# State-space layer of a two-layer trunk: mask products and a sum moved from GpSimd to VectorE, the modulation's running sums divided differently over the groups

## Chip, core and metric

The kernel runs on one core of a Trainium2 chip. The metric is device time in microseconds (us) of one execution. Engines: PE is TensorE, DVE is VectorE, ACT is ScalarE, POOL is GpSimd, SP is SyncE, which here issues DMAs. They run side by side and wait for one another through semaphores; each works off its own instructions strictly in program order.

## What is computed

A trunk of two layers for 512 tokens of width 1024. Each layer makes six rows of modulation from a vector c, runs a mixer and then a mixture of experts. The mixer of the second layer, which the change concerns, is a state-space layer with 8 groups of 4 heads, cut into 4 chunks of 128 tokens:

```
mod = silu(c) @ ada_w[layer] + ada_b[layer]          # shift1, scale1, gate1, shift2, scale2, gate2
z, xbc, dt = split(modulate(rmsnorm(x)) @ w_in)
xs, B, C   = split(silu(conv4(xbc) + conv_b))
x_dt   = xs * softplus(dt + bias);  a_cs = cumsum(dt * A) in each chunk
y_diag = (C B^T * exp(a_cs_l - a_cs_s), lower triangle) x_dt        # the mask product
y_off  = C prev * exp(a_cs)                                         # prev: scan over the chunks' states
y = y_diag + y_off + xs * D                                         # the sum of y's parts
g = y * silu(z);  g = g * rsqrt(mean(g*g over the group's 256) + eps) * norm_w
x = x + gate1 * (g @ w_out)
```

## The kernel before

All of the state-space layer is in `odd_mixer`. A loop over g = 0 to 8 does in each turn the dense products and the convolution of group g and the later steps of group g - 1. Tokens lie along the free axis (512), channels on the partitions; a group has 256 channels of x and z, in two tiles q = 0, 1, and 128 each of B and C.

Of one group, in the order in which the program writes it:

- `conv`: a dense product (pdb, pdc, pdx; 24 matmuls of 128x512 each, since weights and activations are split into a high and a low part, L449 to L452; low parts by L112), then four taps of the convolution: the first on ACT (L1592), three on DVE (L1595, 511, 510 and 509 columns wide), then Silu on ACT (L1598), which may need the loading of a table. The next weights' splits (names b2h, b2l for the B columns of group 2) are made meanwhile.
- `decay` and `masked`: ms, the decays exp(a_cs_l - a_cs_s) for four heads and one chunk, 128x512, on ACT (L1631, L1633); then ms times cbm, the product C B^T under the triangle (L1618). Four of these multiplications a group (L1646): before, chunks 0 and 2 on POOL, 1 and 3 on DVE.
- `xtok`: x turned to tokens on PE (pxd, L1659), times dt (xdt, L1662) and times the decay to the chunk's end (xw, L1665) on DVE.
- `states`: pst on PE (L1673) from xw, and the scan prev on ACT and DVE.
- `ymm`: y_diag into pyd (L1692) and y_off into pyo (L1696) on PE; `zgate`: z and its Silu zt (L1703).
- `assemble`: yy = D x + pyd (L1711, DVE), yt = pyo times the decay (L1714, DVE), yy + yt (L1716, POOL, 128x384), times zt into gT (L1718, L1720, DVE); squares on ACT, and their sum gsum on POOL (L1727).
- `gnorm`, of two groups at a time: pgn (L1733, PE, sums over channels), gv (L1736, DVE), Ln (L1738) and Exp (L1739) on ACT, each with a table load, three steps on DVE to gy (L1741 to L1743), a broadcast of a row over the partitions, gb, on POOL (L1746), and gT times it on DVE (L1749).

Woven in is the modulation of this layer: a11 and a12 are generators (`ada`) that make columns 2048 to 4095 of mod (gate1, shift2) and 4096 to 6143 (scale2, gate2), here called its two halves. Each keeps a running sum over 8 weight tiles on DVE (L204 the first, L202 the seven others, 128x2048 each) and ends with a row sum on PE (L212), an addition on DVE (L215) and stores by SP (L221, L223); the second half also prepares the router, with reloading mc (L244) and plb on PE (L249). The list `fill` holds their 20 steps in order, and OFILL[g] says how many are taken at the end of group g; what is left runs at the end of group 7.

After that `gate_row` loads gate1 (L463) into the same buffer (tag "rows", one buffer) that the second half's rows occupied. `out_proj` multiplies g with w_out in 16 steps of 128 rows: SP loads a step's weight rows (sor, L484) two steps ahead, DVE scales them by the gate (L492), ACT and DVE split them (sow0h, sow0l and so on, L111, L112) and g (gs), and PE adds up 24 products (so, L457 to L459). With it come expert weights for the next part on the same SP queue.

What sets the order of instructions: they are written in the order above, and a scheduler with estimated durations then orders each engine's program; tables on ACT are kept in order by explicit dependencies (`in_order`). The trace's order is thus the program's order and not one made on the chip.

Of the kernel before, what the change touches and what calls it, by code (L numbers as in the profile page):

```python
# [20 lines left out]
P = 128  # L21
# [38 lines left out]
NTMP = 2  # L60
TAIL = 2
FILL = (0, 1, 5, 0, 1, 0, 1, 1, 1, 2, 1, 0, 0, 1, 0, 5, 4, 0, 0, 1, 1, 1, 4, 0, 12)
OFILL = (4, 0, 5, 4, 4, 0, 3, 4)
LO = {"v": "V", "e": "VVG", "m": "V", "o": "V", "s": "VV"}
FPOOL = (0,)
FSTEPS = "x0 h0 x1 h0 x2 h1 h1 h1 h0 x3 h2 h2 h3 h2 h3 h3"
# [10 lines left out]
def trunk_kernel(ctx, tc, x, c, ada_w, ada_b, norm1_w, norm2_w, mix_w_in, pool_w, pool_scale,  # L77
# [4 lines left out]
    V, S, GP, PE, SP = nc.vector, nc.scalar, nc.gpsimd, nc.tensor, nc.sync  # L82
# [1372 lines left out]
    def odd_mixer(layer, prev):  # L1455
        with ExitStack() as es:
# [25 lines left out]
            with ExitStack() as es2:  # L1482
# [92 lines left out]
                gs = [dict() for _ in range(G)]  # L1575

                def tmp(name):
                    return gp.tile([P, T], F32, tag="tmp", name=name, bufs=NTMP)
# [64 lines left out]
                def masked(g, cq):  # L1643

                    ms = gs[g]["ms", cq]
                    (V if cq % 2 else GP).tensor_mul(ms, ms, gs[g]["cbm"][:, cq, None, :].to_broadcast([P, 4, P]))  # L1646

                def xtok(g):

# [58 lines left out]
                def assemble(g, q):  # L1708
                    d = gs[g]
                    y = gp.tile([P, T], F32, tag="yy", name=f"yy{g}{q}", bufs=2)  # L1710
                    V.scalar_tensor_tensor(y, d["x", q], dcol[:, 2 * g + q:2 * g + q + 1],  # L1711
                                           d["pyd"][q].rearrange("p c l -> p (c l)"), op0=ALU.mult, op1=ALU.add)
                    t = tmp(f"yt{g}{q}")
                    V.tensor_mul(t[:, P:], d["pyo"][q][:, 1:, :].rearrange("p c l -> p (c l)"),  # L1714
                                 d["eb"][:, q, 1:, :].rearrange("p c l -> p (c l)"))
                    GP.tensor_add(y[:, P:], y[:, P:], t[:, P:])  # L1716
                    if g + q:
                        V.tensor_mul(gT[2 * g + q], y, d["z", q])  # L1718
                    else:
                        V.scalar_tensor_tensor(gT[2 * g + q], y, 0.5, d["z", q], op0=ALU.mult, op1=ALU.mult)  # L1720
                    if q == 0:
                        s = d["s"] = gp.tile([P, T], F32, tag="gsum", name=f"gsum{g}", bufs=2)
                        S.activation(s, gT[2 * g], AF.Square)
                    else:
                        t = tmp(f"sq{g}")
                        S.activation(t, gT[2 * g + 1], AF.Square)
                        GP.tensor_add(d["s"], d["s"], t)  # L1727
# [27 lines left out]
                for g in range(G + 1):  # L1755
# [26 lines left out]
                    if g:  # L1782
                        assemble(g - 1, 0)
                        assemble(g - 1, 1)
                    if d is not None:
                        if g == 0:
                            next(dt)
                            zgate(g, 0)
                            next(dt)
                            exps(g)  # L1790
                        cbt(g)
                        if g:
                            zgate(g, 0)
                        zgate(g, 1)
                        xtok(g)
                        for cq in range(NT):
                            masked(g, cq)
                        for _ in range(OFILL[g]):
                            if fill:
                                next(fill.pop(0), None)  # L1800
# [76 lines left out]
```

## Time and profile before

| | us |
|---|---|
| runs | 1082.63, 1078.89, 1082.91 |
| median of the runs | 1082.63 |
| profiled execution, its own time | 1078.06 |
| span of its instructions | 1076.4 |
| mean granted clock of TensorE in it | 0.969 |
| PE busy | 975.1 |
| DVE busy | 667.7 |
| ACT busy | 440.6 |
| POOL busy | 219.9 |
| the state-space layer, about | 470 to 820 |

The profile comes from one execution, whose own time is 1078.06 us; its span leaves out the 1.7 us before the first and after the last instruction. Busy shares are averages over all stages: PE is the busiest engine, so time is to be sought in the places where PE stands, and a row says behind the waiting instruction which instruction on which engine it waited for. In rows of a timeline the number ahead is the start in us from the start of the span, the second the duration of the instructions joined in that row, and the bracket at the end the idle time of the engine just before and what ended it.

### The profile page before, as it was taken

The page shows a single profiled execution, that of the slowest core. Times are in us where ns is not written, and L with a number is a line of the kernel's source. Part 1 is how long each engine was busy: PE and PEld are TensorE (multiplying, and loading weights), DVE is VectorE, ACT ScalarE, POOL GpSimd, SP SyncE. Part 2 cuts the span into 40 slices and gives each one's busy share as a digit, 9 for nine tenths or more (in the row PEclk, how much of TensorE's full clock was granted, in tenths as well). Part 3 has the DMA queues.
Part 4 walks back from the last instruction along what each step waited for, and adds up shares of the span by engine and source line. Part 5 has one row for each costly group of instructions (what it writes and reads, how often), then busy time and mean ns, then how long its engine had stood idle before and what let it go on. Part 6 is the DMA issues. An engine that isn't in the chain of part 4 may idle for free. (4 is left out here: it accounts for less than half of the span.)

```text
span 1076.4 us, 15960 instructions
## 1 busy us (share of the span) xinstructions
PE 975.1 (91%) x5700; PEld 718.9 (67%) x5700; DVE 667.7 (62%) x1476; ACT 440.6 (41%) x893; POOL 219.9 (20%) x284
## 2 busy tenths in 40 slices
PE   5799998897899997899899999999969997998994
PEld 4576655686665656777787777878748876665653
DVE  3523443445556875758976699686766655654874
ACT  3434433324223235247475564664723234222332
POOL 3002110305231134200220131121130005221134
PEclk9899999998899999999999999999989998899997
DMA  8689856697799979547764387454236754799987
GB/s 313 240 280 313 287 219 268 243 369 255 234 386 414 409 210 298 187 122 229 236 182 129 107 235 245 127 150 144 79 118 222 267 194 159 261 411 414 411 258 182
DMA packets 137840, 263.88 MB, mean 245 GB/s; under 512 B 17555, under 2 KB 79975, under 8 KB 132632
## 3 DMA queue, kind: packets, MB, share of 16 engines
q1 hardware_dynamic: 126760, 235.36, 62.6%
q0 software_dynamic: 8928, 20.97, 7.4%
q10 hardware_dynamic: 2064, 6.42, 1.5%
q8 instruction: 49, 0.80, 0.3%
q14 instruction: 39, 0.32, 0.1%
HBM read 254.15 MB, written 20.11 MB: 255 GB/s over the span
## 5 line engine op out<-in xcount | busy, mean ns | idle before, releaser
L1063 PE MATMUL ph<-w,xT 128*64 128x256 f32 (+1 forms) x1152 | 132.0, 373 | 1.9 <-DVE xT L1047 1.6
L1063 PEld LDWEIGHTS ph<-w,xT 128*64 128x64 f32 x1152 | 86.4, 139 | 53.1 <-ACT xT L1049 9.5
L1065 ACT ACTIVATE th<-ph 128x128 f32<-128x128 f32 x34 | 9.4, 277 | 154.1 <-PE pht L1074 136.7
L1084 PE MATMUL pyy<-w,hidT 128*64 128x512 f32 x272 | 65.9, 605 | 2.2 <-ACT hidT L1076 2.2
L1030 POOL DMA_INDIRECT xg<-xnd,toks x32 | 32.2, 1007 | 150.8 <-PE pxt L1042 114.8
L1646 POOL TENSOR_TENSOR ms<-ms,cbm 128x512 f32<-128x512 f32 x16 | 27.1, 1709 | 167.9 <-DVE cbm L1618 116.9
L1049 ACT ACTIVATE xT<-pxt,mc 128x128 f32<-128x128 f32 x136 | 51.1, 456 | 17.4 <-PE pxt L1042 11.9
L1089 DVE SCALAR_TENSOR_TENSOR y<-pyy,wsl,gate 128x512 f32<-128x512 f32 x68 | 48.1, 745 | 9.2 <-DMA yd<-y 7.5
L1042 PE MATMUL pxt<-ident,xg 128*128 128x128 f32 x272 | 37.9, 284 | 15.0 <-DVEq L1415 8.6
L1047 DVE TENSOR_SCALAR xT<-pxt,mc 128x128 f32<-128x128 f32 x136 | 46.7, 405 | 1.4 <-PE pxt L1042 1.4
L1042 PEld LDWEIGHTS pxt<-ident,xg 128*128 128x128 f32 x272 | 34.5, 194 | 15.5 <-issue 15.1
L1115 DVE TENSOR_TENSOR x<-x,pyc 128x512 f32<-128x512 f32 x48 | 30.5, 684 | 22.6 <-DMA x<-yd,row 18.3
L1066 DVE SCALAR_TENSOR_TENSOR th<-th,ph 128x128 f32<-128x128 f32 x34 | 9.8, 287 | 55.2 <-ACT th L1065 55.2
L1631 ACT ACTIVATE ms<-lb,acs 128x128 f32<-128x128 f32 x128 | 40.0, 391 | 5.9 <-DMA lb<-acd 5.9
L1716 POOL TENSOR_TENSOR yy<-yy,yt 128x384 f32<-128x384 f32 x16 | 20.0, 1255 | 102.2 <-DVE yt L1714 81.2
L1595 DVE SCALAR_TENSOR_TENSOR cvx<-pdx,cw,cvx 128x511 f32<-128x511 f32 (+2 forms) x48 | 35.6, 742 | 2.4 <-ACT cvx L1592 2.2
L1210 POOL DMA_INDIRECT x<-yd,row x16 | 26.0, 1623 | 49.6 <-issue 24.0
L1084 PEld LDWEIGHTS pyy<-w,hidT 128*64 128x64 f32 x272 | 16.5, 136 | 26.0 <-issue 19.4
L202 DVE SCALAR_TENSOR_TENSOR ada<-ada,ccol,ada 128x2048 f32<-128x2048 f32 x14 | 33.6, 2403 | 0.1
L492 DVE TENSOR_TENSOR sor<-sor,gate 128x1024 f32<-128x1024 f32 x16 | 19.5, 1223 | 21.4 <-DMA sor<-in_ssm_w_out_dram 21.4
L1107 PE MATMUL pyc<-yh,yot 128*128 128x512 f32 x96 | 25.8, 397 | 2.9 <-DVE yot L1097 2.9
L168 PE MATMUL pada<-ada,ccol 128*32 128x512 f32 x192 | 24.9, 600 | 1.0 <-DMA ada<-in_ada_w_dram 1.0
(1087 smaller groups left out, 2667.4 us busy)
## 6 DMA issues: line engine op xcount, KB each, us to landing
w<-in_moe_w_dram SPq DMA_DIRECT2D x192, 512.0 KB
ada<-in_ada_w_dram SPq DMA_DIRECT2D x40, 1024.0 KB
yd<-y SPq DMA_DIRECT2D x22, 512.0 KB
ada<-in_ada_w_dram SPq DMA_DIRECT2D x16, 512.0 KB
wx<-in_ssm_w_in_dram SPq DMA_DIRECT2D x16, 512.0 KB
wz<-in_ssm_w_in_dram SPq DMA_DIRECT2D x16, 512.0 KB
lb<-acd SPq DMA_DIRECT2D x32, 256.0 KB
sor<-in_ssm_w_out_dram SPq DMA_DIRECT2D x16, 512.0 KB
```

The lines of the kernel that those rows point to most:

```text
L202: a = eng.scalar_tensor_tensor(ws[k], ws[k], ccol[:, k:k + 1], ws[k - 1], op0=ALU.mult, op1=ALU.add)
L1030: d = GP.indirect_dma_start(out=xg, out_offset=None, in_=xnd[:, :], in_offset=bass.IndirectOffsetOnAxis(ap=idx, axis=0), bounds_check=T - ...
L1042: PE.transpose(p[:, q, :], xv[:, 4 * hf + q, :], ident)
L1047: V.tensor_scalar(xT[:, k, :], p[:, q, :], a, b, op0=ALU.mult, op1=ALU.add)
L1049: S.activation(xT[:, k, :], p[:, q, :], AF.Identity, bias=b, scale=a)
L1063: PE.matmul(ph[64 * j:64 * j + 64, n:n + h, :], xT[:, k, 64 * j:64 * j + 64], w13[n][:, :, k, :], start=k == 0, stop=k == KD - 1, skip_gro ...
L1084: PE.matmul(py[64 * j:64 * j + 64], hT[:, 64 * j:64 * j + 64], w2[:, s], start=True, stop=True, skip_group_check=True)
L1089: V.scalar_tensor_tensor(y[:, s], py, self.wsl[:, slot:slot + 1], self.gate2[:, s], op0=ALU.mult, op1=ALU.mult)
L1115: V.tensor_add(xst["x"][i][:, s], xst["x"][i][:, s], p)
L1595: V.scalar_tensor_tensor(a[:, sh:], p[:, :T - sh], cw[:, tap, ch:ch + 1], a[:, sh:], op0=ALU.mult, op1=ALU.add)
L1631: S.activation(ms[:, h, :], lb[:, h, :], AF.Relu, scale=-1.0, bias=acs[:, cq, 4 * g + h:4 * g + h + 1])
L1646: (V if cq % 2 else GP).tensor_mul(ms, ms, gs[g]["cbm"][:, cq, None, :].to_broadcast([P, 4, P]))
```

## The change

The mask products all go to DVE, the sum yy + yt goes to DVE, and the 20 steps of the running sums are taken as 2, 3, 3, 3, 3, 3, 2, 2 instead of 4, 0, 5, 4, 4, 0, 3, 4. The first half of the modulation then ends in group 3 in both; the second half ended in group 6 and now ends in group 7.

```diff
--- before.py
+++ after.py
@@ -60,7 +60,7 @@
 NTMP = 2
 TAIL = 2
 FILL = (0, 1, 5, 0, 1, 0, 1, 1, 1, 2, 1, 0, 0, 1, 0, 5, 4, 0, 0, 1, 1, 1, 4, 0, 12)
-OFILL = (4, 0, 5, 4, 4, 0, 3, 4)
+OFILL = (2, 3, 3, 3, 3, 3, 2, 2)
 LO = {"v": "V", "e": "VVG", "m": "V", "o": "V", "s": "VV"}
 FPOOL = (0,)
 FSTEPS = "x0 h0 x1 h0 x2 h1 h1 h1 h0 x3 h2 h2 h3 h2 h3 h3"
@@ -1643,7 +1643,7 @@
                 def masked(g, cq):
 
                     ms = gs[g]["ms", cq]
-                    (V if cq % 2 else GP).tensor_mul(ms, ms, gs[g]["cbm"][:, cq, None, :].to_broadcast([P, 4, P]))
+                    V.tensor_mul(ms, ms, gs[g]["cbm"][:, cq, None, :].to_broadcast([P, 4, P]))
 
                 def xtok(g):
 
@@ -1713,7 +1713,7 @@
                     t = tmp(f"yt{g}{q}")
                     V.tensor_mul(t[:, P:], d["pyo"][q][:, 1:, :].rearrange("p c l -> p (c l)"),
                                  d["eb"][:, q, 1:, :].rearrange("p c l -> p (c l)"))
-                    GP.tensor_add(y[:, P:], y[:, P:], t[:, P:])
+                    V.tensor_add(y[:, P:], y[:, P:], t[:, P:])
                     if g + q:
                         V.tensor_mul(gT[2 * g + q], y, d["z", q])
                     else:
```

On DVE, around the convolution of x in group 1; ada is the running sum, cvx the taps, ms the masks, b2l and c2l the low parts of the next weights. Before:

```order
L1646 TENSOR_TENSOR ms_5240<-ms_5240,cbm_5324 128x512
L1646 TENSOR_TENSOR ms_5256<-ms_5256,cbm_5324 128x512
L202 SCALAR_TENSOR_TENSOR ada_5069<-ada_5069,ccol,ada_5066 128x2048
L1595 SCALAR_TENSOR_TENSOR cvx_5293<-pdx_5268,cw,cvx_5293 128x511
L112 TENSOR_TENSOR b2l<-wb_5262,b2h 128x1024
L1595 SCALAR_TENSOR_TENSOR cvx_5293<-pdx_5268,cw,cvx_5293 128x510
L112 TENSOR_TENSOR c2l<-wc_5332,c2h 128x1024
L1595 SCALAR_TENSOR_TENSOR cvx_5293<-pdx_5268,cw,cvx_5293 128x509
L202 SCALAR_TENSOR_TENSOR ada_5072<-ada_5072,ccol,ada_5069 128x2048
L202 SCALAR_TENSOR_TENSOR ada_5075<-ada_5075,ccol,ada_5072 128x2048
```

and after:

```order
L1646 TENSOR_TENSOR ms_5226<-ms_5226,cbm_5318 128x512
L1595 SCALAR_TENSOR_TENSOR cvx_5287<-pdx_5262,cw,cvx_5287 128x511
L1646 TENSOR_TENSOR ms_5234<-ms_5234,cbm_5318 128x512
L1595 SCALAR_TENSOR_TENSOR cvx_5287<-pdx_5262,cw,cvx_5287 128x510
L1646 TENSOR_TENSOR ms_5242<-ms_5242,cbm_5318 128x512
L1595 SCALAR_TENSOR_TENSOR cvx_5287<-pdx_5262,cw,cvx_5287 128x509
L112 TENSOR_TENSOR b2l<-wb_5256,b2h 128x1024
L112 TENSOR_TENSOR c2l<-wc_5326,c2h 128x1024
L1646 TENSOR_TENSOR ms_5250<-ms_5250,cbm_5318 128x512
L202 SCALAR_TENSOR_TENSOR ada_5069<-ada_5069,ccol,ada_5066 128x2048
```

Two masks more stand here; three stand between or ahead of the taps, the sum ahead of the taps and the splits between them have moved behind the last tap (509 columns), and one sum instead of two stands there.

On PE, where the second half's row sum (pada, L212) and the router's product (plb, L249) stand; pxd are the turned x, b7h the B columns of group 7. Before, between the steps of groups 6 and 7:

```order
L1659 MATMUL pxd_7199<-ident,cvx_7083 128x128
L212 MATMUL pada_7213<-ada_6509,ones 32x512 x4
L249 MATMUL plb_7224<-wr_6139,mc_6140 128x40 x8
L449 MATMUL pdb_7241<-sh_hi,b7h 128x512
L451 MATMUL pdb_7241<-sh_lo,b7h 128x512
```

and after, in group 7 behind its own turned x and ahead of its states:

```order
L1659 MATMUL pxd_7546<-ident,cvx_7431 128x128
L212 MATMUL pada_7558<-ada_6868,ones 32x512 x4
L249 MATMUL plb_7569<-wr_6139,mc_6140 128x40 x8
L1673 MATMUL pst_7595<-xw_7536,btk_7479 128x256
L1673 MATMUL pst_7598<-xw_7536,btk_7479 128x256
```

Both instructions have moved from ahead of group 7's dense products to behind them.

On ACT, at the last norm (gy) and the beginning of the output projection; sow0h, sow1h, sow2h are the high parts of its first weights, gs those of g, gsum and sq the squares. Before:

```order
L1723 ACTIVATE gsum_7638<-gT_5080 128x512
L1726 ACTIVATE sq_7646<-gT_5080 128x512
L1738 ACT_TABLE_LOAD
L1738 ACTIVATE gy_7654<-gv_7652 128x512
L111 ACTIVATE sow2h<-sor_7741 128x1024
L1739 ACT_TABLE_LOAD
L1739 ACTIVATE gy_7654<-gy_7654 128x512
L111 ACTIVATE gs_7794<-gT_5077 128x512
```

and after:

```order
L1723 ACTIVATE gsum_7638<-gT_5074 128x512
L1726 ACTIVATE sq_7646<-gT_5074 128x512
L1738 ACT_TABLE_LOAD
L1738 ACTIVATE gy_7654<-gv_7652 128x512
L111 ACTIVATE sow0h<-sor_7705 128x1024
L1739 ACT_TABLE_LOAD
L1739 ACTIVATE gy_7654<-gy_7654 128x512
L111 ACTIVATE gs_7714<-gT_5071 128x512
```

The split of the third weights stood between Ln and Exp, and now that of the first stands there, since the splits of the first two weights and two of g, which were made before this norm, now follow it.

## Rows read from the trace of the kernel before

**Rows 1.** The page, part 1: engine, busy us, share of the span, instructions.

```profile
PE 975.1 (91%) x5700; PEld 718.9 (67%) x5700; DVE 667.7 (62%) x1476; ACT 440.6 (41%) x893; POOL 219.9 (20%) x284
```

**Rows 2.** Stretches: us, busy of PE, PEld, DVE, ACT, POOL; clock, DMA share, GB/s.

```profile
514.00:557.00 43.00, 39.76 (x211) 32.39 (x211) 38.90 (x46) 24.59 (x45) 6.04 (x5) 1.00 0.77 234
773.00:805.00 32.00, 22.64 (x111) 16.19 (x110) 25.07 (x38) 9.34 (x16) 11.48 (x10) 0.84 0.31 105
```

**Rows 3.** PE's waits, 430 to 830: us in total, times, longest.

```profile
PE pst L1673 <- DVE xw L1665: 7.8, 3, 6.6
PE pxd L1659 <- ACT cvx L1598: 3.2, 1, 3.2
...
PE pyo L1696 <- ACT zt L1703: 2.1, 3, 1.4
...
PE pdx L449 <- DVE cvb L1595: 1.1, 1, 1.1
```

**Rows 4.** Durations in ns, min/median/max, of tiles and lines; yt from DVE's timeline.

```profile
L1646 POOL TENSOR_TENSOR ms<-ms,cbm x16: 1286/1741/2281, 483.0 to 774.5; 128x512 f32<-128x512 f32 x16
L1646 DVE TENSOR_TENSOR ms<-ms,cbm x16: 673/1234/1791, 485.9 to 777.4; 128x512 f32<-128x512 f32 x16
...
L1716 POOL TENSOR_TENSOR yy<-yy,yt x16: 980/1003/3038, 509.0 to 798.9; 128x384 f32<-128x384 f32 x16
...
L202 DVE SCALAR_TENSOR_TENSOR ada<-ada,ccol,ada x14: 2337/2344/3165, 493.1 to 666.6; 128x2048 f32<-128x2048 f32 x14
...
797.98 0.56 DVE L1714 TENSOR_TENSOR yt<-pyo,eb 128x384 f32<-128x384 f32 x1
```

**Rows 5.** DVE's, then ScalarE's timeline around group 1's taps: start us, duration, idle before.

```profile
514.03 3.48 DVE L1646 TENSOR_TENSOR ms<-ms,cbm 128x512 f32<-128x512 f32 x2
...
523.28 0.73 DVE L1595 SCALAR_TENSOR_TENSOR cvx<-pdx,cw,cvx 128x509 f32<-128x509 f32 x1
...
524.10 1.28 ACT L1598 ACT_TABLE_LOAD   x1 [6.75 <-DVE cvx L1595]
```

**Rows 6.** Timelines of DVE and POOL at two norms; last, DVE at 783.

```profile
602.10 1.13 DVE L1743 SCALAR_TENSOR_TENSOR gy<-gv,gy 128x512 f32<-128x512 f32 x1
...
608.49 0.80 POOL L1746 PARTITION_BROADCAST gb<-gy  x1 [5.81 <-issue]
...
813.27 0.80 POOL L1746 PARTITION_BROADCAST gb<-gy  x1 [9.99 <-DVE gy L1743]
...
783.13 1.42 DVE L1749 SCALAR_TENSOR_TENSOR gT<-gT,vcol,gb 128x512 f32<-128x512 f32 x2 [2.69 <-POOL gb L1746]
```

**Rows 7.** PE's timeline, group 7 and the layer's end.

```profile
737.03 1.06 PE L212 MATMUL pada<-ada,ones 128*32 128x512 f32 x8
...
739.84 0.48 PE L449 MATMUL pdb<-sh_hi,b7h 128*128 128x512 f32 x1
...
788.37 2.90 PE L1673 MATMUL pst<-xw,btk 128*128 128x256 f32 x6 [6.62 <-DVE xw L1665]
...
799.01 0.50 PE L457 MATMUL so<-sow0h,gs 128*128 128x512 f32 x1
...
803.33 1.07 PE L1733 MATMUL pgn<-gsum,ones 128*64 128x512 f32 x2 [1.53 <-POOL gsum L1727]
```

**Rows 8.** Splits at the end: DVE's timeline, then ScalarE's last gs.

```profile
789.47 1.22 DVE L112 TENSOR_TENSOR sow1l<-sor,sow1h 128x1024 fp32r<-128x1024 f32 x1
...
790.94 0.69 DVE L112 TENSOR_TENSOR gs<-gT,gs 128x512 fp32r<-128x512 f32 x1
...
810.29 0.62 ACT L111 ACTIVATE gs<-gT 128x512 fp32r<-128x512 f32 x1
```

**Rows 9.** The gate row of layer 0: SP's load and DVE's first use.

```profile
180.98 0.33 SPq L463 DMA_DIRECT2D gate<-modd  x1
...
185.24 1.23 DVE L492 TENSOR_TENSOR mor<-mor,gate 128x1024 f32<-128x1024 f32 x1 [3.43 <-DMA gate<-modd]
```

**Rows 10.** Stretch behind the wait of group 7's pst, columns as in rows 2.

```profile
786.00:792.00 6.00, 3.63 (x14) 2.66 (x16) 5.96 (x14) 0.90 (x2) 0.00 (x0) 0.50 0.42 113
```

## The prediction, made before the changed kernel was run

> **What bounds the kernel now.** I read the busy shares first: TensorE (PE) works 975.1 us of the profiled span, 91%, against 667.7 us for DVE and 219.9 us for POOL [rows 1]. So less work on POOL, or more on DVE, matters only where PE stands waiting for it. The stretch table shows where that is. Inside a group of the state-space layer (514 to 557 us) PE is busy 39.8 of 43 us and DVE 38.9, so DVE has little air there; at the layer's end (773 to 805 us) PE is busy only 22.6 of 32 us at a mean granted clock of 0.84, and DVE 25.1 [rows 2]. Then the list of PE's waits between 430 and 830 us: pst waits 7.8 us for xw, of which one wait is 6.6 us; pxd 3.2 us for the conv of x; pyo 2.1 us in three waits for the gate z; pdx 1.1 us for the taps of B [rows 3]. DVE stands behind all of them, directly or through ScalarE. That is the pot from which this change can pay.
>
> **Masks and adds, from POOL to DVE.** A mask multiply takes a median of 1.74 us on POOL and 1.23 us on DVE, but the shortest on DVE is 0.67 us [rows 4]; the long ones run beside a POOL operation. The sum of y takes 1.00 us on POOL for 128x384; on DVE I take 0.56 us, from the product yt of the same shape [rows 4]. DVE gains 16 x 0.67 + 16 x 0.56 = 19.7 us of work, and gets back 16 x (1.23 - 0.67) = 9.0 us on the masks that it already had, and part of the time in which it waited for POOL's sums. At worst it is 19.7 us busier, at best some 8, over 350 us and eight groups: 1 to 2.5 us a group. In the groups that were fullest the moved running sums weigh more, next.
>
> **Running sums, spread.** Fourteen multiply-adds of 2.34 us [rows 4], and the two that begin the sums, move among the groups. Group 1 matters most: before, two masks (3.48 us together) and a sum (2.34) stand ahead of its taps, and the last tap of x starts at 523.28, behind which ScalarE ends an idle time of 6.75 us [rows 5]; PE then waits the 3.2 us of pxd. In the new order no sum stands ahead of that tap, and the masks take 0.67 us each, three of them between the taps. Against the old order that is 2.34 + 3.48 - 3 x 0.67 = 3.8 us less, and the two splits of B and C for the next group (1.2 us each [rows 8]) stand behind the last tap instead of between: 6.2 us sooner, less 1.1 for the two sums of y. So the 3.2 us wait goes, with 1.9 us over. The taps of B, for which pdx waited 1.1 us, lose the sum that stood between the x taps of the group before; I let that wait go too. Groups 2 and 4 take up the sums: walking DVE's new order against PE's there I find 1.4 to 2.9 us of air, so no new wait, though little is needed for one.
>
> **POOL's broadcasts.** In the norm at 602 us gy ends at 602.10 + 1.13 = 603.23 and the broadcast starts at 608.49, after 5.81 us in which POOL waits for nothing that the profile shows; a mask had held it until then. In the last norm, where POOL had stood 9.99 us, the broadcast starts as soon as gy is there [rows 6]. So some 6 us pass between a POOL tensor operation and a broadcast, and they are hidden if POOL is free that long. With the masks gone, the operation ahead of the broadcast is gsum, long before. DVE, which waited 2.69 us for the broadcast at 783 [rows 6], and in the same way in the norms of the groups before, then waits for none. Where xw follows the broadcast it comes as much sooner, and the small waits of pst (7.8 - 6.6 = 1.2 us) and those of pyo (2.1 us) vanish.
>
> Upstream sum: 1.1 + 3.2 + 1.2 + 2.1 = **7.6 us** of PE waits. It can be as little as 3.2 (group 1 alone is cured) and not more than 7.6, since no other wait of PE in these groups hangs on DVE or POOL.
>
> **The row sum and router matmuls of the modulation's second half** (L212, L249) go from ahead of group 7's dense products, where PE is full, into the wait before pst of group 7. They occupy PE from 737.03 to 739.84, **2.8 us** [rows 7]. At the new place they cost nothing while PE would idle there anyway: 6.6 us before, and by the next part still 3 or more.
>
> **The end of the layer.** Before, the broadcast of the norm of groups 4 and 5 lets DVE go on at 783.13 [rows 6], pst starts at 788.37 and the last pgn at 803.33 [rows 7]. After, the 2.7 us wait is gone, and a scaling of weight rows by the gate (1.2 us), the lo part of the weights (1.2) and a split of g (0.7) [rows 8, 9] have moved behind the last norm, so xw is ready 5 us sooner, near 783. PE, with the 2.8 us ahead of pst, starts it near 784.5. From pst to pgn took 15.0 us; another lo part and split (1.9 us) and DVE's waits for POOL's sum (1 us) leave it, so pgn comes near 796.5, 7 us sooner. But before, PE had products of the output projection to run from 799.01 [rows 7], because their weights had been split ahead. Around pgn it lost 1.5 us of wait and 1.0 of pgn's matmuls, so that start is worth 801.5 without interruption. After, the first weights are split on ScalarE between Ln and Exp of the last norm, and gs behind Exp. The same chain ran in the trace from pgn at 803.33 [rows 7] to the end of gs at 810.29 + 0.62 = 810.9 [rows 8]: 7.6 us. So the first product starts at 796.5 + 7.6 = 804.1: **2.6 us lost**, not 7 won.
>
> The gate row is loaded later too, since its buffer holds the second half's rows until these are stored, now in group 7 instead of ahead of it. In layer 0 the load issued at 180.98 let DVE start at 185.24, 4.2 us [rows 9]. With the row sum at 783 and its operations behind it I put its landing near 794, while the scaling is wanted near 797: 3 us of cover.
>
> [...]
>
> The sum, against the profiled execution's 1078.06 us: -7.6 - 2.8 + 2.6 + 2.0 = -5.8, that is 1072.3 us, 0.54% less. The median of the three runs lies 4.6 us above the profiled execution, the mean of all four 2.6 above it; with 2.7 added the forecast is **1075 us**.
>
> **Rivals**, each against the same 1078.06 first, then with the 2.7 us.
> (a) *The end, or a group, takes more back.* With nothing split ahead DVE owes each of 16 steps 1.2 (scaling) + 1.2 (lo of the weights) + 0.7 (split of g) = 3.1 us [rows 8, 9], while PE needs about 24 x 39.76/211 = 4.5 us [rows 2]; the first two or three steps have under 1 us of margin. Two waits of 1 us and 1 us more of clock give -5.8 + 3 = -2.8; a wait of 3 us in group 2 or 4, where the sums now crowd, gives the same: 1078, no change to be told (a measurement of this kernel can tell about 0.5%, 5.4 us, from no change). For it speaks how full DVE was (38.9 of 43), against it that DVE has no conv at the end.
> (b) *More is won*: the clock does not fall and ScalarE's chain is shorter by the split that need not stand in it: -7.6 - 2.8 + 0 = -10.4: 1070.
> (c) *The output projection starves.* The weight rows of step 4 are now loaded behind three expert-weight loads on the SP queue, and the gate has other loads ahead. If the gate lands 6 us late beyond its cover and the rows of step 4 cost another 6, the sum is -5.8 + 12 = +6: 1087. It decides when the gate lands after 797. Against it: the DMA engines were busy 31% between 773 and 805 [rows 2].
> (d) *The 6 us before the broadcast are not hidden*, because they begin only once gy is there. Then each in-loop norm is as late as before; DVE stands 2.7 us in two of them again, which takes back the 1.2 and 2.1, and in group 7 xw is 2.7 us later and more DVE work lies ahead of it: -5.8 + 3.3 + 2.7 + 2.5 (a wait like that in group 1 at the added DVE work) = +2.7: 1083. Against it is 813.27 [rows 6].
> [...]
>
> **Chances.** Forecast 0.46, of which I count 0.30 below the 0.5% line and 0.16 above it, as the sum lies so near; (a) 0.22; (b) 0.14; (c) 0.12; (d) 0.06. The range runs from below (b), 1067, to above (d), 1084; outside lie (c) and little else. Faster by over 0.5%: 0.30 + 0.14 = 0.44. Within 0.5%: 0.16 + 0.22 + 0.03 = 0.41. Slower by over 0.5%: (c) and a heavier (d), 0.15.
>
> **What would show it.** In the new trace: no wait of pxd in group 1; the broadcast within 1 us behind gy in the in-loop norms; pst of group 7 behind L249 with a wait of 1 to 2 us; 7 to 8 us from the last pgn to the first product, with the clock near 0.5 around it. It is wrong if DVE's masks take 1.2 us without POOL beside them, if the broadcast still starts 5 us behind gy, if a new wait of PE stands in group 2 or 4, or if a wait for the gate or for weight rows stands ahead of the projection.

## The result, and the profile of the changed kernel

Six runs of the changed kernel gave 1065.00 to 1069.53 us, median 1067.64; six of the kernel before 1077.51 to 1082.91, median 1080.34. The ratio is 0.9886 with a 95% interval of 0.9865 to 0.9907: 12.3 us less (10 to 14.6). The forecast was 1075 us and, as a sum, 5.8 us less: the right side, and less than half of the size. The time lies at the very low end of the range that was stated, 1067 to 1084 us.

The busy line of the changed kernel's page (columns as in [rows 1]):

```profile
PE 975.3 (91%) x5700; PEld 722.0 (68%) x5700; DVE 671.4 (63%) x1508; ACT 441.1 (41%) x893; POOL 175.4 (16%) x252
```

Two stretches of the layer's end in it (columns as in [rows 2]):

```profile
776.00:782.00 6.00, 0.79 (x5) 0.52 (x4) 3.90 (x9) 1.23 (x2) 1.18 (x1) 0.72 0.77 287
782.00:790.00 8.00, 1.97 (x2) 0.29 (x2) 4.43 (x5) 5.06 (x6) 0.08 (x1) 0.50 0.00 0
```

DVE is busy only 3.7 us longer than before although it took over 32 operations, and POOL 44.5 us shorter. PE's busy time is the same. At the end of the layer PE now stands longer than before: 2.8 us of work in the 14 us from 776 to 790, and the clock is at 0.50 when the products of the projection begin.

PE's waits between 430 and 820 us (columns as in [rows 3]):

```profile
PE so L457 <- ACT gs L111: 6.2, 1, 6.2
PE pgn L1733 <- POOL gsum L1727: 5.0, 1, 5.0
...
PE pyo L1696 <- DVE prev L1681: 0.3, 1, 0.3
```

One row of the same list of the kernel before (columns as in [rows 3]):

```profile
PE pgn L1733 <- POOL gsum L1727: 2.7, 2, 1.5
```

Of the four rows of [rows 3] nothing is left: pst waits for no xw, pxd for no cvx, pdx for no tap, and one wait of 0.3 us stands at a pyo. At the very end the opposite has happened: the waits of the last pgn for gsum, two of 2.7 us together before, have become one of 5.0 us, and the first product now waits 6.2 us for ACT's gs.

The masks of the changed kernel, by tile (columns as in [rows 4]):

```profile
L1646 DVE TENSOR_TENSOR ms<-ms,cbm x32: 674/684/1178, 482.1 to 770.8; 128x512 f32<-128x512 f32 x32
```

The sums of y, by tile:

```profile
L1716 DVE TENSOR_TENSOR yy<-yy,yt x16: 546/551/559, 507.9 to 778.3; 128x384 f32<-128x384 f32 x16
```

A mask on DVE takes 0.68 us in the median instead of 1.23, since 22 of the 32 have no POOL operation beside them now (the longest, 1.18 us, runs beside gsum); the sum takes 0.55 instead of 1.00 on POOL.

The last tap of x in group 1 on DVE's timeline, to be held against [rows 5]:

```profile
515.00 0.73 DVE L1595 SCALAR_TENSOR_TENSOR cvx<-pdx,cw,cvx 128x509 f32<-128x509 f32 x1
```

The norm at 596 us on POOL's timeline, to be held against [rows 6]:

```profile
596.07 0.80 POOL L1746 PARTITION_BROADCAST gb<-gy  x1 [43.39 <-DVE gy L1743]
599.15 1.63 POOL L1746 PARTITION_BROADCAST gb<-gy  x1 [2.27 <-DVE gT L1749]
608.42 2.15 POOL L1727 TENSOR_TENSOR gsum<-gsum,sq 128x512 f32<-128x512 f32 x1 [7.65 <-issue]
```

The layer begins 1.2 us sooner here than in the profile before (group 0's turned x at 478.9 against 480.1), so the last tap of x comes 523.28 - 515.00 - 1.2 = 7.1 us sooner, counted from the start of the layer. The broadcast starts as soon as gy lets it. But behind the second broadcast POOL again passes 7.65 us in which it waits for nothing that the profile shows, before the next tensor operation, gsum. Nobody is waiting for that one at this place.

Group 7 and the layer's end on PE's timeline, to be held against [rows 7]:

```profile
767.07 1.06 PE L212 MATMUL pada<-ada,ones 128*32 128x512 f32 x8
...
769.87 1.88 PE L1673 MATMUL pst<-xw,btk 128*128 128x256 f32 x6
...
782.13 1.97 PE L1733 MATMUL pgn<-gsum,ones 128*64 128x512 f32 x2 [5.03 <-POOL gsum L1727]
790.29 0.79 PE L457 MATMUL so<-sow0h,gs 128*128 128x512 f32 x1 [6.19 <-ACT gs L111]
```

ACT's chain behind the last pgn, its timeline, to be held against [rows 8]:

```profile
784.90 1.28 ACT L1738 ACT_TABLE_LOAD   x1 [4.17 <-DVE gv L1736]
...
786.74 1.04 ACT L111 ACTIVATE sow0h<-sor 128x1024 fp32r<-128x1024 f32 x1
...
789.62 0.61 ACT L111 ACTIVATE gs<-gT 128x512 fp32r<-128x512 f32 x1
```

The row sum (L212) now runs in front of pst, and pst follows without a bracket, that is without a wait. From the last pgn to the first product stand 8.2 us: gv on DVE, then ACT's table load, Ln, the split sow0h, the second table load, Exp and gs, one behind the other.

### The profile page after: what moved, and what is told of

Read it like the earlier page. It is cut to its first block, busy times and chain, and to the rows that moved or that the text cites. A ratio compares the mean times of both kernels' runs of the same rounds, so it can differ in the third digit from the quotient of the medians.

```text
span 1067.8 us, 15932 instructions
## 1 busy us (share of the span) xinstructions
PE 975.3 (91%) x5700; PEld 722.0 (68%) x5700; DVE 671.4 (63%) x1508; ACT 441.1 (41%) x893; POOL 175.4 (16%) x252
## 5 line engine op out<-in xcount | busy, mean ns | idle before, releaser
L1049 ACT ACTIVATE xT<-pxt,mc 128x128 f32<-128x128 f32 x136 | 51.1, 457 | 17.3 <-PE pxt L1042 11.8
L1727 POOL TENSOR_TENSOR gsum<-gsum,sq 128x512 f32<-128x512 f32 x8 | 11.7, 1458 | 188.6 <-ACT sq L1726 166.2
L1084 PEld LDWEIGHTS pyy<-w,hidT 128*64 128x64 f32 x272 | 16.5, 136 | 28.3 <-issue 19.4
L1746 POOL PARTITION_BROADCAST gb<-gy x8 | 9.2, 1151 | 147.6 <-DVE gy L1743 139.0
```

What stands on the lines that cost most here:

```text
L1049: S.activation(xT[:, k, :], p[:, q, :], AF.Identity, bias=b, scale=a)
L1084: PE.matmul(py[64 * j:64 * j + 64], hT[:, 64 * j:64 * j + 64], w2[:, s], start=True, stop=True, skip_group_check=True)
```

## Where the time went, by stretches

The first turned x of group 0 (pxd), that of group 7, the first product of the projection (so) and the last one at L457 are marks that stand in every version. Between the two profiles:

| stretch, us | before | changed | difference |
|---|---|---|---|
| groups: pxd of group 0 to pxd of group 7 | 480.1 to 780.6: 300.5 | 478.9 to 766.1: 287.2 | -13.3 |
| end: to the first so, its interruption of 2.5 by pgn counted before | 20.9 | 24.2 | +3.3 |
| projection: first so to that last one, without that interruption | 96.1 | 98.2 | +2.1 |
| all else | 658.9 | 658.2 | -0.7 |

Together -8.6 us of span (1076.4 to 1067.8). The groups one by one are the turns from one pxd to the next.

Two of these turns in the kernel before, as stretches (columns as in [rows 2]):

```profile
607.10:651.40 44.30, 42.35 (x222) 33.37 (x221) 40.16 (x51) 24.90 (x47) 17.59 (x12) 1.00 0.73 216
693.40:736.10 42.70, 41.27 (x215) 33.02 (x214) 32.08 (x46) 25.11 (x46) 11.64 (x10) 1.00 0.45 123
```

The same turns in the changed kernel:

```profile
601.00:642.50 41.50, 41.50 (x223) 33.32 (x222) 36.66 (x56) 25.16 (x46) 4.45 (x4) 1.00 0.57 161
684.00:724.60 40.60, 40.60 (x215) 33.10 (x214) 34.09 (x53) 25.47 (x46) 2.57 (x2) 1.00 0.52 145
```

The first turn went from 44.3 us to 41.5, the second from 42.7 to 40.6; the last, from 736.1 to 780.6, lost the 3.0 us of the row sum and the router products (44.5 to 41.5). In the changed kernel PE is busy through both of them, and through the five others as well. The granted clock was 1.00 in all four rows, so the clock has no part in these differences.

## Experiments: the parts of the change

Ratios are to the kernel before on the same chip. The stretches are those of the table above, from each version's own profile, "end and projection" in one (117.0 us in the kernel before, 122.4 in the changed one).

| kernel | ratio (interval) | groups | end and projection |
|---|---|---|---|
| before, two profiles | | 300.5, 302.1 | 117.0, 117.4 |
| changed, two profiles | 0.9886, 0.9883 | 287.2, 287.3 | 122.4, 122.1 |
| masks and adds | 0.9847 (0.981 to 0.9884) | 291.8 | 112.8 |
| division alone | 1.0028 (1.0005 to 1.0051) | 297.4 | 125.3 |
| masks alone | 0.9902 (0.9865 to 0.9938) | 298.3 | 115.0 |
| adds alone | 0.9969 (0.9946 to 0.9993) | 297.5 | 117.2 |
| masks of groups 3, 5, 7 | 1.0009 (0.9985 to 1.0033) | 305.1 | 115.0 |
| masks of the other groups | 0.9938 (0.9915 to 0.9961) | 296.9 | 116.7 |
| changed, one step to group 6 | 0.9848 (0.9804 to 0.9891) | 290.3 | 112.7 |
| the same, last gsum on DVE | 0.9833 (0.981 to 0.9856) | 290.4 | 111.0 |
| the same, norm behind xtok in group 7 | 0.986 (0.9813 to 0.9906) | 290.3 | 116.3 |
| before, division ending in group 6 | 0.9964 (0.9942 to 0.9986) | 300.5 | 116.5 |

What lies outside these stretches took between 653.5 and 658.9 us in these profiles, so the ratio of a kernel and the stretches of its one profile can part by some us.

**Masks and adds without the new division.**

```diff
-OFILL = (2, 3, 3, 3, 3, 3, 2, 2)
+OFILL = (4, 0, 5, 4, 4, 0, 3, 4)
```

> The changed kernel with the old division of the running sums (4, 0, 5, 4, 4, 0, 3, 4): masks and the sum of y on DVE only. Theory A (the gain is waits of PE behind DVE, and the masks' leaving POOL removes them; the division only moves the row sum and the end): the waits in groups 1, 3, 4 and 5 go as in the changed kernel, about -10 us; the weights of the output projection are split ahead of the last norm as before, so the end gains about 4 us instead of losing; together -14 us, ratio 0.987. Rival B (the even division carries half of the gain, because DVE has no room for masks, adds and four or five sums in one group): new waits of pxd or pst of 2 to 4 us in groups 2 to 4, together -5 us, ratio 0.995.

Measured 0.9847: faster than the whole change, though the intervals touch; in the profiles the two stretches together take 404.7 us against 409.6. The groups become 8.7 us shorter without the division, and the end and projection 4.2 us shorter where the changed kernel's are 5.4 longer. Rival B falls: DVE has room. Of PE's waits in the groups only that of pdx is left, the one that the prediction had the division cure (PE's timeline):

```profile
492.52 0.50 PE L449 MATMUL pdx<-sh_hi,x10h 128*128 128x512 f32 x1 [1.16 <-DVE cvb L1595]
```

**The division alone.**

```diff
-OFILL = (4, 0, 5, 4, 4, 0, 3, 4)
+OFILL = (2, 3, 3, 3, 3, 3, 2, 2)
```

> The kernel before with the new division of the running sums (2, 3, 3, 3, 3, 3, 2, 2) and nothing else. Theory A: the row sum and the router product hide in the wait of group 7's pst, -3 us; the waits of PE in groups 1, 3, 4, 5 stay, as masks on POOL still hold up DVE and the broadcast; the first product of the projection follows the last norm by 8 us instead of running ahead of it, +8 to +9 us and 2 for the clock: together about +6 us, ratio 1.006. Rival B: the spread removes group 1's wait and half of the others, -5 us, ratio 0.995.

Measured 1.0028. The wait of group 1 stays, and is longer than before. The end and projection take 125.3 us, 8.3 more than before and 2.9 more than in the changed kernel, without the masks to pay for it (PE's timeline):

```profile
524.57 1.54 PE L1659 MATMUL pxd<-ident,cvx 128*128 128x128 f32 x6 [3.96 <-ACT cvx L1598]
...
803.78 0.80 PE L457 MATMUL so<-sow0h,gs 128*128 128x512 f32 x1 [3.30 <-ACT gs L111]
```

DVE's, ahead of that wait:

```profile
515.93 2.34 DVE L202 SCALAR_TENSOR_TENSOR ada<-ada,ccol,ada 128x2048 f32<-128x2048 f32 x1
518.20 0.73 DVE L1595 SCALAR_TENSOR_TENSOR cvx<-pdx,cw,cvx 128x511 f32<-128x511 f32 x1
```

The third part of the change, by itself, is a small loss. It does not move what stands ahead of group 1's taps: two masks (3.49 us) and a sum (2.34) are there as in the kernel before. With masks and adds moved and the old division, the run above, no sum stands ahead of these taps and the wait is gone. So the new order of group 1 comes with the masks and adds, and not with the division; what the sum's place alone is worth there, this run does not show. The turn of group 1 took 47.3 us (43.8 before), also because the granted clock was 0.50 in a stretch behind the wait (last section); three other turns became 1.3 to 1.8 us shorter each.

**Masks alone, adds alone.**

```diff
-(V if cq % 2 else GP).tensor_mul(ms, ms, ...)
+V.tensor_mul(ms, ms, ...)
```

> The kernel before with all masks on DVE; the sum of y stays on POOL, the division is the old one. Theory A: groups 1, 3, 4 and 5 lose their waits, as the masks do this and not the adds, -9 to -10 us, and the end gains 3: ratio 0.988. [...] Rival B: -3 us or less, ratio 0.997.

```diff
-GP.tensor_add(y[:, P:], y[:, P:], t[:, P:])
+V.tensor_add(y[:, P:], y[:, P:], t[:, P:])
```

> The kernel before with only the sum of y moved to DVE; masks and division as before. Theory A (the adds help only once the masks are gone, since the mask is what holds the broadcast and doubles DVE's mask): -2 us, ratio 0.998, the waits of groups 3 to 5 stay. Rival E (the parts add up, and the adds are worth what lies between masks alone at 0.990 and masks with adds at 0.985): -6 us, ratio 0.9945.

Measured 0.9902 and 0.9969. The masks alone meet theory A's ratio, and the adds alone are nearer to theory A's 0.998 than to rival E's 0.9945, which lies just outside the interval. By ratio the two parts add up within the intervals (0.98 + 0.31 = 1.29% against 1.53% together). But in the groups of these profiles the masks alone gave 2.2 us, where theory A had 9 to 10, the adds alone 3.0, and both 8.7. With the masks alone the old waits go and others come, two of them behind prev on DVE; behind the wait of 2.74 us for cvb PE's work in that turn took 1.4 us longer, with its matmuls 0.42 to 0.43 us apart five times in a row instead of 0.23 (last section).

With masks alone, PE's timeline:

```profile
494.01 0.80 PE L449 MATMUL pdx<-sh_hi,x10h 128*128 128x512 f32 x1 [2.74 <-DVE cvb L1595]
...
620.89 0.50 PE L449 MATMUL pdx<-sh_hi,x40h 128*128 128x512 f32 x1 [1.95 <-DVE prev L1681]
```

POOL's timeline there:

```profile
597.89 0.80 POOL L1746 PARTITION_BROADCAST gb<-gy  x1 [43.38 <-DVE gy L1743]
600.97 1.63 POOL L1746 PARTITION_BROADCAST gb<-gy  x1 [2.27 <-DVE gT L1749]
610.11 1.95 POOL L1716 TENSOR_TENSOR yy<-yy,yt 128x384 f32<-128x384 f32 x2 [7.51 <-DVE adab L215]
```

The broadcast at 597.89 is on time now, and the sum of y, which stands behind it on POOL, starts at 610.11, 7.51 us after the second broadcast. DVE's next step, the product with zt, stands 1.42 us for it, and prev and the taps stand behind that on DVE. What POOL had lost ahead of the broadcast it now loses behind it. The bracket names DVE's adab as the releaser, but that operation is not an input of the sum; the next experiments show what the time is.

## Experiments: what POOL loses, and where

**Masks off POOL only where a norm broadcasts, and only elsewhere.**

```diff
-(V if cq % 2 else GP).tensor_mul(ms, ms, ...)
+(V if cq % 2 or g in (3, 5, 7) else GP).tensor_mul(ms, ms, ...)
```

> The kernel before with all masks on DVE in groups 3, 5 and 7 alone, the groups in whose turn a norm broadcasts. Theory A (a mask on POOL makes the broadcast 6 us late): the broadcast follows gy within 1 us, the waits behind it go in groups 4 and 6 and pst of group 7 is 4 to 5 us sooner, while group 1's wait of 3.2 us stays: -8 us, ratio 0.9925. [...]

The other one has `g not in (3, 5, 7)`.

> The kernel before with all masks on DVE in groups 0, 1, 2, 4 and 6, those without a norm; in 3, 5 and 7 as before. Theory A: group 1's wait of pxd goes, the broadcasts stay 5 us behind gy, and the waits in groups 4, 6 and 7 stay: -4 us, ratio 0.9965. [...]

The first gave 1.0009: theory A as I had put it falls. A like gain from each mask, 6 of 16 of the 0.98% of masks alone, would be 0.9963, and lies outside the interval too. The broadcasts were indeed on time and the end gained 2 us, but two waits came into group 4.

PE's timeline there:

```profile
622.26 0.50 PE L449 MATMUL pdx<-sh_hi,x40h 128*128 128x512 f32 x1 [1.98 <-DVE prev L1681]
...
653.83 1.54 PE L1659 MATMUL pxd<-ident,cvx 128*128 128x128 f32 x6 [5.06 <-ACT cvx L1598]
```

POOL's:

```profile
602.62 1.32 POOL L1746 PARTITION_BROADCAST gb<-gy  x1 [2.58 <-DVE gT L1749]
611.47 1.96 POOL L1716 TENSOR_TENSOR yy<-yy,yt 128x384 f32<-128x384 f32 x2 [7.53 <-DVE adab L215]
```

DVE's, ahead of the second wait:

```profile
641.79 3.49 DVE L1646 TENSOR_TENSOR ms<-ms,cbm 128x512 f32<-128x512 f32 x2
645.20 2.34 DVE L202 SCALAR_TENSOR_TENSOR ada<-ada,ccol,ada 128x2048 f32<-128x2048 f32 x1
647.46 0.74 DVE L1595 SCALAR_TENSOR_TENSOR cvx<-pdx,cw,cvx 128x511 f32<-128x511 f32 x1
```

The wait of 1.98 us again follows on the sum of y, 7.53 us behind the broadcast: DVE's product with zt stood 1.45 us for it. The wait of 5.06 us is group 1's wait of the kernel before in another group: the new order of DVE puts two masks (3.49 us, beside POOL's) and a running sum (2.34) ahead of the taps of group 4, whose first now starts at 647.46. In the kernel before these taps stood ahead of the masks. The masks elsewhere gave 0.9938, not theory A's 0.9965, which lies outside the interval, but what a like gain from each mask would be for 10 of 16, 0.9939. In the profile group 1's wait is gone, and one of pst's small waits too; pdx's, pyo's two for zt and the 6.4 us of pst in group 7 are left. Since such a share fails in the first of the two runs, a like gain from each mask does not hold. So the gain of an edit here depends on which side of the taps the scheduler lets the masks fall, and on both sides of the broadcast; the second is argued from the rows above, and POOL's price is tested next.

**POOL's price by itself.** Nine extra operations on scratch tiles in group 2 of the changed kernel, where POOL has only one gsum to do:

```diff
+GP.memset(t0, 1.0)
+GP.tensor_add(t0, t0, t0)
+GP.partition_broadcast(t1, t0[0:1, :])
+GP.partition_broadcast(t1, t0[64:65, :])
+GP.tensor_add(t0, t0, t1)
+GP.tensor_add(t0, t0, t1)
+GP.partition_broadcast(t1, t0[0:1, :])
+GP.memset(t0, 1.0)
+GP.partition_broadcast(t1, t0[0:1, :])
```

> The changed kernel with nine extra POOL operations in group 2, on two scratch tiles that nobody reads: memset, add, broadcast, broadcast, add, add, broadcast, memset, broadcast, one behind the other. Read are only the gaps on POOL. Theory A (POOL pays 6 to 7 us whenever it goes from a tensor operation to a broadcast, and the same on the way back): gaps of 6 to 7 us ahead of the first broadcast, the second add and the third broadcast, none between like operations; the time is longer where scratch tiles hold up others, which is not the question. Rival H (only the way to a broadcast is dear, and what follows it waits for something else): gap ahead of the broadcasts alone. Rival I (it is a price of the first use): gap ahead of the first broadcast alone.

POOL's timeline there (L1803 to L1811 are the added lines in order; columns as in [rows 6]):

```profile
549.80 1.30 POOL L1727 TENSOR_TENSOR gsum<-gsum,sq 128x512 f32<-128x512 f32 x1 [1.29 <-ACT sq L1726]
557.01 0.80 POOL L1805 PARTITION_BROADCAST sw<-sw  x1 [5.92 <-issue]
557.91 0.80 POOL L1806 PARTITION_BROADCAST sw<-sw  x1
565.62 2.24 POOL L1807 TENSOR_TENSOR sw<-sw,sw 128x512 f32<-128x512 f32 x1 [6.92 <-issue]
567.94 1.36 POOL L1808 TENSOR_TENSOR sw<-sw,sw 128x512 f32<-128x512 f32 x1
575.38 0.80 POOL L1809 PARTITION_BROADCAST sw<-sw  x1 [6.08 <-issue]
576.24 0.53 POOL L1810 MEMSET sw<- 128x512 f32 x1
576.86 0.79 POOL L1811 PARTITION_BROADCAST sw<-sw  x1
```

5.92 us ahead of the first broadcast, none ahead of the second, 6.92 us ahead of the next addition, none ahead of the one behind it, 6.08 us ahead of the third broadcast. A memset between two broadcasts costs nothing. So POOL pays 5.92 to 6.92 us at each of these changes between a tensor operation and a broadcast, in both directions, and neither H nor I holds. What the price is made of, no run here shows. The one run of this kernel took 1064.75 us, no longer than the changed one.

## Experiments: the layer's end

**One step of the sums from group 7 to group 6.**

```diff
-OFILL = (2, 3, 3, 3, 3, 3, 2, 2)
+OFILL = (2, 3, 3, 3, 3, 3, 3, 1)
```

> The changed kernel with one step of the running sums moved from group 7 to group 6 (2, 3, 3, 3, 3, 3, 3, 1), so that the second half ends in group 6 and the gate's buffer is free as early as before. Theory A: the row sum and router product stand again ahead of group 7's dense products, +3 us against the changed kernel, but weights are split ahead of the last norm and products of the projection run between: the 10 us that the end gave back between pst of group 7 and the first product are won but for 2 to 3, and the clock does not fall: together -4 to -5 us against the changed kernel, ratio to before 0.985. Theory D (the end is bound by DVE's work there, not by the order of its instructions): no gain, +3 us, ratio 0.992.

Measured 0.9848, against 0.9886 and 0.9883 of the changed kernel; in the profile the groups take the 3.1 us of the row sum again, and the end and projection are 9.7 us shorter. Theory D falls. Against the old division with masks and adds moved, 0.9847, it gives nothing that the runs can tell. What is left of PE's waits ahead of the first product, its timeline:

```profile
771.03 2.90 PE L1673 MATMUL pst<-xw,btk 128*128 128x256 f32 x6 [4.20 <-DVE xw L1665]
```

The first product runs at 779.2, 13.4 us after group 7's pxd instead of 24.2, and pgn interrupts it. The same division in the kernel before, with masks and adds on POOL as they were:

```diff
-OFILL = (4, 0, 5, 4, 4, 0, 3, 4)
+OFILL = (2, 3, 3, 3, 3, 3, 3, 1)
```

> The kernel before with only the division 2, 3, 3, 3, 3, 3, 3, 1, in which the second half ends in group 6 as before. Theory A (what the even division costs is the end's order, because the gate's buffer is free too late): against the even division of the change alone (1.003) it gains back 5 to 8 us: ratio 0.997. Rival B' (the even division itself is bad while masks contend with DVE): ratio 1.002 or more.

Measured 0.9964, against 1.0028 of the division alone: some 7 us from one step, as theory A had it (5.7 us of it in the stretches of the two profiles). So what the change's own division costs is that the second half of the modulation ends one group too late.

**The last sums of squares on DVE** (on top of that step):

```diff
-GP.tensor_add(d["s"], d["s"], t)
+(V if g >= G - 2 else GP).tensor_add(d["s"], d["s"], t)
```

> The changed kernel with one step of the sums moved to group 6, as before, and the sum of squares gsum of groups 6 and 7 on DVE. Theory A: the last two pgn no longer wait 1.3 us for POOL, and DVE does in 0.7 us what took POOL 2.1 to 2.8 us: -1.5 to -2 us against the version without it, ratio to before 0.983. Rival G (DVE is the limit at the layer's end and the sum delays its other work there): 0 to +1 us, ratio 0.985 to 0.986.

Measured 0.9833, the fastest version (median 1059.77 us). The wait of pgn that was left, 1.3 us, is gone and the end and projection are 1.7 us shorter, near the expectation; by the runs alone, 0.9848 and 0.9833, the two can't be told apart.

**The norm behind the turned x in group 7** (on top of both):

```diff
-while norm:
+while norm and g < G - 1:
     run(norm.pop())
 ...
     masked(g, cq)
+while norm:
+    run(norm.pop())
```

> The version with one step moved to group 6 and the last sums of squares on DVE, and in group 7 the norm of groups 4 and 5 written behind that group's turned x instead of ahead. Theory A (the 4.2 us wait of pst in group 7 that is left is DVE's norm work standing ahead of xw in its program): xw comes 3 to 4 us sooner, -3 us, ratio to before 0.980. Theory D (the end is bound by the amount of DVE's work, and what is moved out of the way is late elsewhere): no gain, ratio 0.983.

Measured 0.986. The longest wait of pst shrank only from 4.2 to 3.3 us, and the projection paid for it (PE's timeline):

```profile
796.28 0.79 PE L457 MATMUL so<-sow2h,gs 128*128 128x512 f32 x1 [2.78 <-ACT gs L111]
```

The third step of the projection waits 2.8 us for gs, and the end and projection take 116.3 us instead of 111.0. Here theory D is the better one: what is put off at this place is late elsewhere. By the ratios alone, 0.986 and 0.9833, the two can't be told apart.

**A second profile of both kernels.** The runs differ by 12.3 us, the two profiles by 8.5.

> The kernel before once more, for a second profile beside a second one of the changed kernel from the same chip and call. Theory J (the 3 to 4 us by which the runs' difference, 12.3 us, exceeds that of the two profiles, 8.5, lie ahead of the layer and change from one execution to the next): the layer from group 0's turned x to the projection's last product takes 417.5 us again within 1, and the start of the layer lies between 473 and 480 us. Rival K (the layer itself varies): more than 2 us of difference inside the layer.

> The changed kernel once more. Theory J: 409.6 us for the same stretch within 1, the start of the layer between 473 and 480, ratio 0.988 to 0.992. Rival K: more than 2 us of difference inside the layer; ratio below 0.988 with a shorter layer.

The repetitions gave 1.0003 and 0.9883. The layer, from group 0's turned x to the last product at L457, took 419.4 and 409.4 us (417.5 and 409.6 in the first profiles), and it began at 476.9 and 477.4 (480.1 and 478.9). So neither J nor K as put: the layer of the kernel before varies by 2 us, the changed one's hardly. The trace shows where 1.5 us of these 2 lie: behind nearly the same wait in group 1 (3.24 and 3.16 us) the granted clock stayed at 1.00 in the first profile and was 0.50 in the second, and the turn took 43.8 and 45.3 us (rows in the last section). Inside the layer 8 to 10 us are seen; the 2 to 4 us by which the runs differ more stay open. Part of them is which execution was profiled: both profiles of the kernel before lie 2.1 to 2.3 us below the median of its runs, and the first of the changed kernel, 1069.53 us, is the slowest of its six.

## Why the prediction was too small

- **Group 1, pdx, pst, pyo: -7.6 us predicted.** All these waits went. But the turns became shorter by 13.3 - 3.0 = 10.3 us. This is the mis-sized step, "Upstream sum" and its "not more than 7.6": I priced the waits by the idle time in their brackets. The brackets of the kernel before sum up to 7.7 us in these turns; the other 2.6 us stand in the rows as PE's busy time, for the most part. In the two turns shown PE was busy 42.35 us for 222 instructions before and 41.50 for 223 after; and 41.27 and 40.60 for 215 each. A dense matmul's row is 0.39 us long where the next one starts 0.23 us later, so a short hold lies inside the row and shows no bracket. In the kernel before the six pst ahead of group 4's C columns (c4h) led to the next matmul after 1.42 us, in the changed one after 1.10, both without a bracket.

PE's timeline before:

```profile
614.73 1.77 PE L1673 MATMUL pst<-xw,btk 128*128 128x256 f32 x6
616.15 0.58 PE L449 MATMUL pdc<-sh_hi,c4h 128*128 128x512 f32 x1
```

PE's timeline in the changed kernel:

```profile
608.54 1.46 PE L1673 MATMUL pst<-xw,btk 128*128 128x256 f32 x6
609.64 0.58 PE L449 MATMUL pdc<-sh_hi,c4h 128*128 128x512 f32 x1
```

- **A price of these waits that stands nowhere in the sum.** I charged the clock at the layer's end alone. In the second pair of profiles the turns became 302.1 - 287.3 - 3.0 = 11.8 us shorter, 1.5 us more than in the first, since there the clock had fallen behind group 1's wait (0.50, last section). How often that happens in the runs without a profile is not shown.
- **Where group 1's wait came from.** The order that I read off the changed program was right, and its last tap came 7.1 us sooner where I had 6.2 - 1.1 = 5.1. But I put it down to the division of the sums, and there the text was wrong: with the division alone the sum stands ahead of the taps as before and the wait stayed, 3.96 us; with masks alone, adds alone and masks off POOL outside the norms it went. With the adds alone a sum still stands between the taps (at 509.07). So it is what stands ahead of the last tap on DVE altogether, and how long it takes, that decides. The division cured pdx's 1.1 us, as the run without it shows.
- **DVE's load.** 8 to 19.7 us more were reckoned, 3.7 were measured: the 32 masks take 23.1 us (19.4 for 16 before), the sums 8.5, and the products with zt at L1718 went from 14.3 to 9.9 us. For this I had no term.
- **Broadcasts.** That they would follow gy at once, and DVE's waits vanish, was right (11.7 us before, 3.5 in the changed kernel), and rival (d) fell. The prediction missed the way back: the change from broadcast to sum costs as much (7.51 us with the masks alone), and the adds' leaving POOL is what keeps that off DVE. I had counted the adds as load on DVE alone.
- **Row sum and router.** 2.8 us predicted, 3.0 measured.
- **The end.** In the times of the profile before (14.5 us later than the changed kernel's, by group 7's pxd): pst predicted at 784.5, measured 784.4; last pgn 796.5 and 796.6; first product 804.1 and 804.8; loss 2.6 and 3.3. The chain of 7.6 us took 8.2. That pgn agrees to 0.1 us is luck in part: between xw and pgn DVE also did 1.5 us of the modulation's second half (L215, L250, L222), which my sum left out, and no longer did the product with zt of group 6 (2.1 us), which now stands ahead of xw. The wait of 1 to 2 us that I named as a sign at pst did not come: its xw was ready before PE was. The gate was in time: DVE's first scaling, at 784.74, has no wait ahead of it but stands behind gv in DVE's order.
- **The clock.** The 2.0 us in the sum were an estimate of mine, and no run shows such a term by itself; what the profiles show in its place is a projection that took 2.1 us longer and a granted clock of 0.50 from 782 to 790 and still from 791 to 795, in the first products (columns as in [rows 2]):

```profile
791.00:795.00 4.00, 4.00 (x11) 3.13 (x10) 4.00 (x6) 0.70 (x2) 1.12 (x1) 0.50 0.45 146
```

- **Sum.** -13.3 + 3.3 + 2.1 - 0.7 = -8.6 in the profile, where I had -7.6 - 2.8 + 2.6 + 2.0 = -5.8. With 10.3 in place of 7.6 the sum would have been -8.5. What the runs show beyond, up to 12.3, I can't place but for the draw of the profiled executions, above.
- **Rivals.** (a), (c) and (d) did not come: PE has no wait in groups 2 and 4, and none on weight rows or the gate. (b) has the right size only by the runs; its mechanism, a clock that stays up and a shorter chain, is not what happened.

## To carry to other kernels

Price a wait of PE by the distance from one matmul's start to the next, compared with the same instructions where nothing holds them, not by the idle column alone; here the column held three quarters of it. On an engine that pays for changing the kind of its work, as POOL did here with 5.92 to 6.92 us, look at what stands behind the dear operation as well as ahead of it, and move both or neither. When work is spread evenly, look at when the last piece ends and what only then becomes free: one step later cost 7 us here by the runs, and the spreading that ended in time gave 4 (0.9964).

## What the runs showed of the hardware

- In the run with the added operations POOL passed 5.92 and 6.08 us between a tensor operation and a broadcast and 6.92 us the other way, and 0.1 us or less between like operations or on either side of a memset between two broadcasts. In the layer of the kernel before it is 5.81 to 6.05 us at the three norms inside the loop, where a mask is the operation ahead, and 6.90 to 7.19 us the other way; 7.32 to 7.65 us the other way in the changed kernel. It begins when POOL is done with the operation before, not when the inputs come: at 608.49 the broadcast came 5.3 us behind its gy, and in the last norm, where POOL had stood 9.99 us, 0.15 us behind it [rows 6]. In the changed kernel, where POOL had stood 11.45 to 43.39 us, all four came 0.14 to 0.15 us behind their gy. So a POOL that had stood that long hid it.
- The same mask took 0.67 to 0.69 us on DVE alone and up to 1.79 us beside a POOL operation [rows 4]; 32 masks with little of POOL beside them kept DVE busy 23.1 us, 16 before 19.4.
- After a wait of 3.24 us at pxd of group 1 the granted clock was 1.00, and the following matmuls started 0.23 us apart. In the second profile of the same program, after one of 3.16 us at the same place, it was 0.50, and the starts were 0.42 to 0.43 us apart eight times in a row. After one of 3.96 us there, with the division alone, it was 0.50 and they were so eight times too, and after one of 2.74 us at pdx, with the masks alone, five times. So the length of the wait does not order them. The stretches behind the wait (columns as in [rows 2]), in the two profiles of the kernel before and with the division alone:

```profile
527.50:530.40 2.90, 2.90 (x14) 2.42 (x13) 2.90 (x7) 0.44 (x1) 0.00 (x0) 1.00 0.92 323
524.30:527.20 2.90, 2.90 (x8) 2.30 (x7) 2.90 (x7) 0.51 (x1) 0.00 (x0) 0.50 1.00 360
526.30:529.70 3.40, 3.40 (x9) 2.64 (x8) 3.40 (x9) 0.13 (x1) 0.00 (x0) 0.50 0.92 359
```

- Two executions' profiles of the same program differ by 3 us in where the layer starts (480.1 and 476.9), ahead of all that was changed.
- In the two profiles of each kernel PE's instructions, by line and tile, stand in one and the same order from the first to the last. The first profiles of the two kernels show the same for what runs ahead of the first instruction that the change moves on each engine: 2791 instructions on PE, 731 on DVE, 409 on ACT and 156 on POOL.
